# Another layout for the scratch tensor of the routing weights: pieces of four expert rows

## The chip, the cores and the metric

The kernel runs on one core of a Trainium2 chip. The metric is the device time of one launch in microseconds; several runs are compared by their median. Matrix products run on TensorE (PE), elementwise work on VectorE (DVE) and ScalarE (ACT), row gathers are issued by GpSimd (POOL), and most loads by SyncE (SP). Sixteen DMA engines move the data of all queues.

## The reference

Two transformer blocks over 512 tokens of width 1024, float32: the first with grouped attention, a gated convolution and a PEER layer, the second with sliding-window attention and a gated feed-forward layer. What bears on the change is the PEER layer, a mixture of 16384 experts of one hidden unit each:

```python
q = (xc @ wq).reshape(PEER_CHUNK, PEER_HEADS, 2, PEER_HALF)
s = jnp.einsum('thpd,hpnd->thpn', q, keys)          # 128 x 128 keys
s_top, i_top = lax.top_k(s, PEER_TOPK)              # 16 of each half
...
best_s, best_pos = lax.top_k(cand_s, PEER_TOPK)     # 16 experts of each head
w = jax.nn.softmax(best_s.astype(jnp.float32), axis=-1)
act = jax.nn.gelu(jnp.einsum('thkd,td->thk', jnp.take(u_tab, eid, axis=0), xc), approximate=False)
return jnp.einsum('thk,thkd->td', w * act, jnp.take(v_tab, eid, axis=0))
```

## The kernel before

The experts form a table of 128 rows of 128. For 384 of the 512 tokens (`TD`; `NTD` = 3 tiles of 128) the kernel computes the layer densely: for each expert row `b`, `stage_a` multiplies the tokens with the 128 vectors of the row (24 matmuls of three-part float32 into one PSUM bank of the two of `ps_mm`) and evicts the Gelu of it (`gt<-mm` on ACT), `stage_w` multiplies this with the routing weights of that row, and `stage_y` multiplies with the row's output vectors into the six banks `ys`. The last 128 tokens are done by gathers: GpSimd fetches the rows of `peer_u` and `peer_v` by index, and VectorE does the products.

The routing weights of the dense tokens come from `route` (VectorE) and `spread`. `spread` takes tokens in `NGRP` = 12 groups of `GW` = 32; for each token one matmul of two one-hot matrices gives its 128 x 128 table of weights in PSUM (`r`, the four banks of `ps_r`), and ACT copies these into the two staging tiles `wst[0]` and `wst[1]` (halves of the tile `rows1`, 64 expert rows each; the profile calls them `rows`). After the last eight tokens of a group, ACT issues one write of 1 MB out of each staging tile into the DRAM tensor `wr_d` (line 1357): 24 writes. `wr_d` is needed since the weights are made by tokens and used by expert rows.

This happens while PE also runs `lead(b)`: the first `LEAD` = 76 expert rows' `stage_a`, whose results ACT stores to the DRAM tensor `g_d` (line 1392). PE's matmuls for `spread` stand between those of `stage_a` in an order that is fixed when the program is built, by the costs and due times of the class `Pace`. After that `stage_a` for the other 52 rows and `stage_y` for all run by pairs of rows in the order `DSEQ`. Two steps ahead, `prepare` calls `load_wr(c)`, which loads the weights of `CH` = 4 expert rows for all 12 groups (768 KB, line 1409, two buffers, 32 loads on SyncE), and `load_g(b)`, which loads a stored `stage_a` (line 1414, also SyncE). The u and v tables come by loads of 1 MB each on SyncE (`raw`, line 271). Engines that go through the scheduler all have line 88 in the profile; the tile's name tells them apart.

Of the kernel before, what the change touches and what calls it, by code (L numbers as in the profile page):

```python
# [11 lines left out]
F32 = mybir.dt.float32  # L12
# [16 lines left out]
GW = 32  # L29
# [3 lines left out]
CH = 128 // GW  # L33
# [5 lines left out]
NGRP = TD // GW  # L39
# [25 lines left out]
class Pace:  # L65
# [119 lines left out]
    def need(self, tag, key="V"):  # L185
        for q in self.q[key]:
            while any(x[3] == tag for x in q):
                self.pop(key, q)
# [31 lines left out]
def tile_dit_peer_then_swa_block(ctx, tc, A, out, dbg=None):  # L220
    nc = tc.nc
# [19 lines left out]
    dram = ctx.enter_context(tc.tile_pool(name="dram", bufs=1, space=bass.MemoryType.DRAM))  # L241
# [107 lines left out]
    def later(items, tile, tag=None, first=False, deadline=1e9, key="V"):  # L349
        pace.later(items, tile, tag, 0 if first else 1, deadline, key)  # L350
# [183 lines left out]
    with ExitStack() as mx:  # L534
# [396 lines left out]
        for i in range(16):  # L931
# [18 lines left out]
            dst, c = (sga_d, sgc_d)[i // 8], i // 2 % 4  # L950
# [162 lines left out]


    sm = pool(ctx, "small2", 4)
    wr_d = dram.tile([NGRP, 128, 128 * GW], F32, name="wr_d")
    g_d = dram.tile([LEAD, 128, TD], F32, name="g_d")
    hp_ = ExitStack()
    gp = pool(hp_, "gp")
# [62 lines left out]
    if True:  # L1182
# [160 lines left out]
        def spread(t):  # L1343
            def group(g, g8, oa, ob):
                def f():
                    for u4 in range(2):
                        pw = ps_r.tile([128, 4, 128], F32, name="r", tag="r")
                        for u in range(4):
                            v = 4 * u4 + u
                            PE.matmul(pw[:, u, :], oa[:, v // 2, :, v % 2], ob[:, v // 2, :, v % 2], start=True, stop=True)  # L1350
                        n = 2 * (t * (128 // GW) + g)
                        o = 8 * g8 + 4 * u4
                        for i in range(2):
                            st = wst[i]
                            S.copy(st[:, :, o:o + 4], pw[:, :, i * 64:i * 64 + 64].rearrange("p t i -> p i t"))
                            if o == GW - 4:
                                nc.scalar.dma_start(wr_d[n // 2][:, i * 64 * GW:(i + 1) * 64 * GW],
                                                    st.rearrange("p i t -> p (i t)"))
                return f
            for g in range(128 // GW):  # L1360
                for g8 in range(GW // 8):
                    yield 2.9, lambda: cTs[t][1] if t in cTs else None
                    need(("cT", t), "PE")
                    n = ngrp[0]
                    ngrp[0] += 1
                    need(("oh", n - 2), "PE")
                    ci, cw = cTs[t]
                    oa = rw.tile([128, 4, 128, 2], F32, name="oa", tag="oab", bufs=4)
                    ob = rw.tile([128, 4, 128, 2], F32, name="ob", tag="oab", bufs=4)
                    eq = rw.tile([128, 4, 128, 2], BF, name="eq")  # L1370
                    ts_ = slice(g * GW + g8 * 8, g * GW + g8 * 8 + 8)
                    numbers = iota_u[:, None].to_broadcast([128, 4, 128, 2])

                    def eight(c):
                        return c[:, ts_].rearrange("p (a b) -> p a b", b=2)[:, :, None, :].to_broadcast([128, 4, 128, 2])
                    V.tensor_tensor(eq, numbers, eight(ci[:, 1]), op=ALU.is_equal)
                    V.tensor_tensor(oa, numbers, eight(ci[:, 0]), op=ALU.is_equal)
                    V.tensor_tensor(ob, eq, eight(cw), op=ALU.mult)
                    later([(1.8, group(g, g8, oa, ob))], ob, ("oh", n), key="PE")
# [20 lines left out]
    with ExitStack() as de:  # L1400
# [3 lines left out]
        wr, wfs = {}, {}  # L1404

        def load_wr(c):
            if c not in wr:
                wr[c] = dn.tile([128, NGRP, CH * GW], F32, name="wr", tag="wr", bufs=2)
                nc.sync.dma_start(wr[c], wr_d[:, :, c * CH * GW:(c + 1) * CH * GW].rearrange("g p c -> p g c"))
                pace.load(wr[c])  # L1410

        def load_g(b):
# [39 lines left out]
        def prepare(s):  # L1452

            if s >= steps:
                return
            j = DSEQ[s]
            for b in (2 * j, 2 * j + 1):
                load_wr(b // CH)
                if b < LEAD:
                    load_g(b)  # L1460
# [340 lines left out]
    with ExitStack() as ff:  # L1801
# [4 lines left out]
        for f0, f1 in FH:  # L1806
            f_hi = wk.tile([128, 12, T], F32R, name="f_hi", tag="f_hi", bufs=1)
            f_lo = wk.tile([128, 12, T], F32R, name="f_lo", tag="f_lo", bufs=1)
            for fc in range(f0 // 2, f1 // 2):
# [8 lines left out]
                for b in range(2):  # L1818
                    ps = block_T(uw, b, h_hi, h_lo) if fc else part_T(uw, b, h_hi, h_lo, slice(256, 512), early[2 + b])
                    V.tensor_tensor(sg[b], sg[b], ps, op=ALU.mult)  # L1820
                    i = 2 * fc + b - f0
# [105 lines left out]
```

## Time and profile before

| what | value |
|---|---|
| median of 3 runs | 2504.13 us (2501.92 to 2504.7) |
| the profiled execution, its own time | 2511.68 us |
| its span, first to last instruction | 2509.9 us |
| PE busy | 2417.8 us, 96% |
| VectorE, ACT, GpSimd busy | 71%, 40%, 14% |
| DMA | 491.27 MB, 196 GB/s mean |
| writes of `wr_d` (ACT) | 24 of 1024 KB, 860.1 to 1114.2 us |
| loads of `wr` (SyncE) | 32 of 768 KB, 1118.8 to 1890.8 us |

Times in the rows are microseconds from the start of the span unless ns is said. A row of instructions names the engine, the line, the operation and the tiles as out<-in; `ACTq` and `SPq` are the sequencers that issue DMAs. `q1` is the DMA queue of SyncE, `q10` that of ACT, `q0` that of the gathers. A group's idle time is that of the engine just ahead of it, with what ended it.

### The profile page before, as it was taken

How to read it: one execution, taken by the hardware profiler on the slowest of the kernel's cores; microseconds unless marked ns; L12 is line 12 of the kernel's file. 1: busy time of each engine (PE TensorE's matmuls, PEld its weight loads, DVE VectorE, ACT ScalarE, POOL GpSimd, SP SyncE). 2: the span in 40 equal slices, each digit the busy share in tenths (PEclk: the TensorE clock that was granted, in tenths of full speed). 3: DMA queues.
4: the chain of work that ended last, by engine and by line, in shares of the span. 5: the costliest groups of instructions: out<-in, count | busy, mean ns of one | idle time of the engine just before them, and what ended most of it. 6: DMA issues, size and time to landing. Idle time of an engine off the chain costs nothing. (4 is left out here: it accounts for less than half of the span.)

```text
span 2509.9 us, 33263 instructions
## 1 busy us (share of the span) xinstructions
PE 2417.8 (96%) x12953; PEld 2087.0 (83%) x12953; DVE 1781.7 (71%) x3259; ACT 1011.6 (40%) x1744; POOL 352.4 (14%) x278
## 2 busy tenths in 40 slices
PE   6999999998999999999999999999998999999998
PEld 4887878688899999998888888888887878888887
DVE  3899994555899999875877777778887487333333
ACT  4336556435334444443333333333335365321222
POOL 0000000000001112221433433334420000000000
PEclk9999999999999999999999999999999999999999
DMA  7222234344236677778998999999984211323221
GB/s 271 77 95 92 85 116 141 117 148 144 73 115 239 224 278 264 258 270 302 331 339 308 356 328 350 342 337 341 330 309 133 85 51 51 100 94 101 84 92 59
DMA packets 246318, 491.27 MB, mean 196 GB/s; under 512 B 12432, under 2 KB 177936, under 8 KB 226192
## 3 DMA queue, kind: packets, MB, share of 16 engines
q1 hardware_dynamic: 188032, 301.75, 35.0%
q0 software_dynamic: 36864, 134.23, 14.6%
q10 hardware_dynamic: 21264, 53.16, 5.8%
q8 instruction: 102, 1.67, 0.3%
q14 instruction: 56, 0.46, 0.1%
HBM read 440.60 MB, written 48.50 MB: 195 GB/s over the span
## 5 line engine op out<-in xcount | busy, mean ns | idle before, releaser
L88 DVE TENSOR_TENSOR wlo<-raw,whi 128x1024 fp32r<-128x1024 f32 (+1 forms) x420 | 494.1, 1216 | 236.4 <-ACT whi L88 235.7
L88 PE MATMUL mm<-hx_hi,whi 128*128 128x384 f32 (+2 forms) x1408 | 511.1, 363 | 16.1 <-ACT hx_hi L88 7.3
L88 ACT CAST whi<-raw 128x1024 fp32r<-128x1024 f32 (+1 forms) x420 | 418.3, 1045 | 200.6 <-PE pd L88 68.8
L88 PE MATMUL mm<-hx_lo,whi 128*128 128x384 f32 (+2 forms) x1408 | 497.5, 353 | 1.3 <-DVE hx_lo L88 1.3
L88 PE MATMUL mm<-hx_hi,wlo 128*128 128x384 f32 (+2 forms) x1408 | 496.8, 353 | 1.7 <-DVE wlo L88 1.7
L88 PE MATMUL y<-whi,wf 128*128 128x512 f32 x1536 | 428.3, 397 | 5.3 <-ACT whi L88 5.3
L88 PEld LDWEIGHTS y<-whi,wf 128*128 128x128 f32 x1536 | 288.6, 188 | 74.7 <-ACT whi L88 7.6
L1161 POOL DMA_INDIRECT rows<-in_peer_u_dram,eid x128 | 174.2, 1361 | 914.0 <-DVE eid L88 528.9
L88 PEld LDWEIGHTS mm<-hx_hi,whi 128*128 128x128 f32 x1408 | 267.0, 190 | 33.7 <-ACT hx_hi L88 8.7
L88 PEld LDWEIGHTS mm<-hx_hi,wlo 128*128 128x128 f32 x1408 | 266.7, 189 | 19.1 <-DVE wlo L88 3.3
L88 PEld LDWEIGHTS mm<-hx_lo,whi 128*128 128x128 f32 x1408 | 267.1, 190 | 15.6 <-DVE hx_lo L88 3.6
L88 PE MATMUL y<-wlo,wf 128*128 128x512 f32 x768 | 242.4, 397 | 4.1 <-DVE wlo L88 4.1
L1161 POOL DMA_INDIRECT rows<-in_peer_v_dram,eid x128 | 176.0, 1375 | 354.3 <-DVE yg L88 180.6
L88 PEld LDWEIGHTS y<-wlo,wf 128*128 128x128 f32 x768 | 144.1, 188 | 41.0 <-DVE wlo L88 6.7
L88 ACT CAST wf<-gt 128x384 fp32r<-128x384 f32 x128 | 66.1, 516 | 260.2 <-DVE gt L88 222.8
L88 DVE SCALAR_TENSOR_TENSOR cacc<-g,pcol,cacc 128x512 f32<-128x512 f32 x240 | 165.7, 751 | 0.0
L88 DVE SCALAR_TENSOR_TENSOR yg<-rows,cf,yg 128x1024 f32<-128x1024 f32 x127 | 162.7, 1281 | 0.9
L88 PE MATMUL mm<-h_hi,whi 128*128 128x512 f32 (+1 forms) x416 | 161.3, 388 | 0.0
L88 PE MATMUL mm<-h_lo,whi 128*128 128x512 f32 (+1 forms) x416 | 160.6, 386 | 0.0
L88 PE MATMUL mm<-h_hi,wlo 128*128 128x512 f32 (+1 forms) x416 | 160.6, 386 | 0.0
L88 DVE SCALAR_TENSOR_TENSOR rows<-rows,hg 128x1024 f32<-128x1024 f32 x128 | 154.2, 1220 | 0.0
L88 ACT ACTIVATE gt<-mm 128x384 f32<-128x384 f32 x128 | 63.9, 499 | 219.5 <-PE mm L88 199.7
(330 smaller groups left out, 3751.6 us busy)
## 6 DMA issues: line engine op xcount, KB each, us to landing
raw<-in_uT_dram SPq DMA_DIRECT2D x64, 1024.0 KB
raw<-in_peer_v_dram SPq DMA_DIRECT2D x64, 1024.0 KB
wr_d<-rows ACTq DMA_DIRECT2D x24, 1024.0 KB
wr<-wr_d SPq DMA_DIRECT2D x32, 768.0 KB
raw<-in_w_in_dram SPq DMA_DIRECT2D x22, 1024.0 KB
raw<-in_w_gu_dram SPq DMA_DIRECT2D x22, 1024.0 KB
raw<-in_w_mod_dram SPq DMA_DIRECT2D x18, 1024.0 KB
g_d<-gt ACTq DMA_DIRECT2D x76, 192.0 KB
```

Of the source, the lines that this page charges most:

```text
L88: return f(*a, **kw)
L1161: G.indirect_dma_start(out=r, out_offset=None, in_=A[tab], in_offset=bass.IndirectOffsetOnAxis(ap=eid[:, j:j + 1], axis=0))
```

## The change

`wr_d` gets the index of the piece of four expert rows (32 of them) first, then the partition, then the token group, then the 4 x 32 weights. A load of `wr` then reads one contiguous piece, 6 KB for each partition, where it read twelve runs of 512 bytes. A write of a staging tile goes to 16 pieces, 512 bytes for each partition and piece, where it was one run of 8 KB for each partition. The number and size of the transfers, who issues them and their place in the program are the same.

```diff
-    wr_d = dram.tile([NGRP, 128, 128 * GW], F32, name="wr_d")
+    wr_d = dram.tile([128 // CH, 128, NGRP, CH * GW], F32, name="wr_d")
...
                             if o == GW - 4:
-                                nc.scalar.dma_start(wr_d[n // 2][:, i * 64 * GW:(i + 1) * 64 * GW],
-                                                    st.rearrange("p i t -> p (i t)"))
+                                nc.scalar.dma_start(wr_d[i * 64 // CH:(i + 1) * 64 // CH, :, n // 2, :].rearrange("c p x -> p c x"),
+                                                    st.rearrange("p (c i) t -> p c (i t)", i=CH))
...
         def load_wr(c):
             if c not in wr:
                 wr[c] = dn.tile([128, NGRP, CH * GW], F32, name="wr", tag="wr", bufs=2)
-                nc.sync.dma_start(wr[c], wr_d[:, :, c * CH * GW:(c + 1) * CH * GW].rearrange("g p c -> p g c"))
+                nc.sync.dma_start(wr[c], wr_d[c])
                 pace.load(wr[c])
```

## Rows read from the trace of the kernel before

**Rows 1.** The page, busy time, share and instructions.
```profile
PE 2417.8 (96%) x12953; PEld 2087.0 (83%) x12953; DVE 1781.7 (71%) x3259; ACT 1011.6 (40%) x1744; POOL 352.4 (14%) x278
```
**Rows 2.** Windows; busy PE, PEld, DVE, ACT, POOL (instructions), clock, DMA share, GB/s.
```profile
860.00:1118.00 258.00, 254.24 (x1678) 252.84 (x1677) 226.93 (x305) 114.48 (x263) 46.80 (x29) 1.00 0.72 262
1118.00:1890.00 772.00, 756.27 (x3604) 650.29 (x3603) 591.38 (x761) 269.02 (x375) 288.00 (x214) 0.99 0.90 329
```
**Rows 3.** DMA queues, 1074.5 to 1076.8 us; packets, MB, share of 16 engines.
```profile
q10 hardware_dynamic: 125, 1.02, 106.7%
```
**Rows 4.** DMA queues, 1179.5 to 1181 us.
```profile
q1 hardware_dynamic: 833, 0.42, 99.5%
```
**Rows 5.** Tile `wr_d`: its DMA issues (ns min/median/max), who waited (us, times).
```profile
L1409 SPq DMA_DIRECT2D wr<-wr_d x32: 377/434/1848, 1118.8 to 1890.8; - x32
L1357 ACTq DMA_DIRECT2D wr_d<-rows x24: 326/326/361, 860.1 to 1114.2; - x24
...
  ACT rows L88: 58.6, 19
```
**Rows 6.** Timeline of ACT, 1073.5 to 1083.5 us; start, duration, idle before.
```profile
1073.68 0.33 ACTq L1357 DMA_DIRECT2D wr_d<-rows  x1
...
1074.45 0.33 ACTq L1357 DMA_DIRECT2D wr_d<-rows  x1
1077.68 0.37 ACT L88 COPY rows<-r 128x256 f32<-128x256 f32 x1 [3.26 <-DMA wr_d<-rows]
1082.13 0.93 ACT L88 COPY rows<-r 128x256 f32<-128x256 f32 x3 [4.07 <-DMA wr_d<-rows]
1082.93 0.53 ACT L88 ACTIVATE gt<-mm 128x384 f32<-128x384 f32 x1
```
**Rows 7.** Timeline of ACT behind the second wait of five other pairs.
```profile
869.93 0.93 ACT L88 COPY rows<-r 128x256 f32<-128x256 f32 x3 [2.01 <-DMA wr_d<-rows]
...
906.56 0.53 ACT L88 ACTIVATE gt<-mm 128x384 f32<-128x384 f32 x1
...
983.35 0.52 ACT L88 ACTIVATE gt<-mm 128x384 f32<-128x384 f32 x1
...
1024.48 0.53 ACT L88 ACTIVATE gt<-mm 128x384 f32<-128x384 f32 x1
...
1101.51 0.93 ACT L88 COPY rows<-r 128x256 f32<-128x256 f32 x3 [2.81 <-DMA wr_d<-rows]
```
**Rows 8.** Timeline of PE: the first matmul that needs what ACT freed.
```profile
871.24 0.63 PE L88 MATMUL r<-ob,oa 128*128 128x128 f32 x4
...
909.39 0.42 PE L88 MATMUL mm<-hx_hi,whi 128*128 128x384 f32 x1
...
984.05 0.34 PE L88 MATMUL mm<-hx_hi,whi 128*128 128x384 f32 x1
...
1025.05 0.44 PE L88 MATMUL mm<-hx_hi,whi 128*128 128x384 f32 x1 [0.43 <-ACT gt L88]
...
1083.51 0.44 PE L88 MATMUL mm<-hx_hi,whi 128*128 128x384 f32 x1
...
1102.24 0.63 PE L88 MATMUL r<-ob,oa 128*128 128x128 f32 x4
```
**Rows 9.** Waits, 1118 to 1145 us; us in total, times, longest.
```profile
ACT gt L88 <- DMA wr<-wr_d: 12.2, 1, 12.2
...
PE mm L88 <- ACT gt L88: 5.0, 1, 5.0
```
**Rows 10.** DMA queues, 1127 to 1132 us.
```profile
q0 software_dynamic: 421, 1.54, 75.6%
q1 hardware_dynamic: 477, 0.24, 16.3%
```
**Rows 11.** Waits of DVE, 1145 to 1890 us.
```profile
DVE gt L88 <- DMA gt<-g_d: 28.4, 13, 7.0
```
**Rows 12.** Tile `g_d`: its loads' issues, ns min/median/max.
```profile
L1414 SPq DMA_DIRECT2D gt<-g_d x76: 320/453/6783, 1119.3 to 1900.5; - x76
```

## The prediction

> **What bounds the kernel now.** I read the page first: TensorE (PE) is busy for 96% of the span [rows 1], so a microsecond counts only where it makes PE stand still. Then the table by windows, for the two stretches in which the scratch tensor `wr_d` is used [rows 2]. While it is written (860 to 1118 us) PE is busy 254.24 of 258 us, 3.8 us idle, with the DMA engines at 0.72. While it is read (1118 to 1890 us) PE is busy 756.27 of 772 us, 15.7 us idle, with the DMA engines at 0.90. So the reading stretch has at most 15.7 us to give back, however much faster its loads become, and the writing stretch has next to no idle time of PE: what is lost there shows at once, unless slack between the engines takes it.
>
> Next the view of the tensor itself [rows 5]. The 24 writes are issued by ScalarE (ACT), and ACT is also who waits for them: 58.6 us in 19 waits. The reason is in `spread`: each of the two staging tiles `wst` exists once, so the copy that begins the next group of 32 tokens must wait until the write out of that tile has landed. The 32 loads are issued by SyncE, and their one long waiter is ACT again, 12.2 us at the first of them [rows 9].
>
> Third, one pair of writes on ACT's timeline [rows 6]: first write issued at 1073.68, second at 1074.45; the first copy of the next group gets its tile at 1077.68 after 3.26 us of idling, the second at 1082.13 after 4.07 more. So 8.45 us pass from the first issue to the end of the second wait. Behind that copy stands the Gelu eviction at 1082.93, and PE starts its next block, in the bank that this eviction frees, at 1083.51 [rows 8]. The eviction ended at 1083.46: the slack is 0.05 us. This reading, who on PE comes right behind the second wait and with how much room, is the one that decides the case, so I made it for all twelve pairs. Six are shown [rows 7, 8]; the copies of `rows` there are three in 0.93 us, so the first ends some 0.4 us after its start:
> - pair of 860 us: copy ends about 870.3, PE's `r` matmul at 871.24: 0.9 us
> - pair of 898 us: Gelu ends 907.09, PE at 909.39: 2.3 us
> - pair of 974 us: 983.87 against 984.05: 0.2 us
> - pair of 1014 us: 1025.01 against 1025.05, and PE has already idled 0.43 us for it: 0.05 us
> - pair of 1073 us: 0.05 us
> - pair of 1091 us: about 1101.9 against 1102.24: 0.35 us
>
> The other six have 2.8 us or more, or no copy waiting.
>
> **The change part by part.** *Writes.* A write of 1 MB went out as 128 packets of 8 KB, eight for each of the 16 DMA engines; now it is 2048 packets of 512 bytes, 128 for each. The price of both sizes is in the trace, in windows where nothing else runs. 8 KB writes: 125 packets at 106.7% of 16 engines over 2.3 us, so 314 ns each [rows 3]. 512-byte packets, of the old loads: 833 at 99.5% over 1.5 us, so 28.7 ns each [rows 4]. Per KB that is 39 against 57 ns. A pair of writes therefore takes 2 x 8 x 314 ns = 5.0 us of every engine before and 2 x 128 x 28.7 ns = 7.35 us after: 2.3 us more. That reads are as dear as writes is assumed; no 512-byte write stands in the trace.
>
> How much later does the second wait end? Of the 8.45 us, 5.0 are the pair's own transfer and 3.4 are the start, the landing and others' packets. If those 3.4 stay, the wait ends 2.3 us later; if all of it grows with the transfer (7.35/5.0), 3.9 us later. The row gathers on the third queue go on all through the stretch, so a longer window catches more of them, but start and landing don't grow: I take 3.0. The issue itself gets dearer: a three-level pattern took 434 ns (the old loads) against 326 for the plain one [rows 5], 0.1 us for each of two writes. So the wait ends 3.2 us later, between 2.5 and 4.1.
>
> Queued behind the waiting copy on ACT are the other copies of that group, the Gelu evictions, their `g_d` stores and the `whi` casts of the next weights; PE waits for the first three kinds as soon as the slack is gone. The shift beyond the slack is then PE's, pair by pair, at 3.2: 2.3 + 0.9 + 3.0 + 3.15 + 3.15 + 2.85 = **15.4 us lost**. At 2.5 it is 11.2; at 4.1 it is 20.8, and 2.3 more from pairs among the other six.
>
> *Loads.* Each load of 768 KB was 1536 packets of 512 bytes and becomes 128 of 6 KB. Between the two prices 6 KB take some 236 ns (an estimate, at the 8 KB packet's rate): 32 loads cost 32 x 96 x 28.7 ns = 88 us of all engines before and 60 after. The 28 us are what the writes gain in length (24 x (128 x 28.7 - 8 x 314) ns = 28 us): the DMA work is moved from the stretch at 0.90 to the one at 0.72, not removed. What the shorter loads release is read from who waited. The large one is the first load, issued at 1118.84 us. From 1127 to 1132 us the gathers (q0) hold 75.6% of the engines with 421 packets, while the queue of the load gets 477 packets through in 16.3% [rows 10]: about one small packet for one of 4 KB. So the load took until about 1138, and ACT stood 12.2 us for it in the middle of its evictions; PE stood 5.0 us [rows 9]. With eight packets of 6 KB for each engine, taken in turn with as many of the gathers, it needs 8 x (0.24 + 0.16) = 3.2 us. That stall goes: **5.0 us gained**. What is late next there is the last pair of writes itself, 3 us later than now, ahead of the first load; the evictions around it held PE up only in that one wait, so I count nothing for it.
>
> After 1145 us the loads of `g_d`, which SyncE issues right behind a load of `wr`, are waited for by VectorE: 28.4 us in 13 waits [rows 11]. No idle time of PE in this stretch is put down to the products behind them; 10.7 us of the 15.7 are left as the cap. I take **1.5 us gained**, between 0 and 10.7.
>
> *Nothing else.* SyncE's own issue gets cheaper (434 to 326 ns, 32 times), hidden, since SyncE mostly waits for free buffers. Computation, tiles and order are untouched.
>
> **Sum.** 15.4 - 5.0 - 1.5 = +8.9 us. The profiled execution took 2511.68 us (span 2509.9 and 1.8 around it); with the change 2520.6. It lies 7.5 us over the median of the runs, 2504.13, and none of that is in these terms, so the forecast for a median is **2513.0 us**.
>
> **The rivals.**
> 1. *Small writes run at the large ones' rate.* Then the waits end 0.2 us later, for the issues alone, PE loses about 0.3 us at the three tightest pairs, and the gains stand: 0.3 - 6.5 = -6.2, 2497.9 us; with the whole idle time of the reading stretch given back, 2489. It decides as soon as the waits grow by less than about 1 us. Against it speak the 28.7 ns: at the large packets' rate 512 bytes would take 19.6 [rows 3, 4]. For it: those were reads, into SBUF.
> The Trainium skill (DMA: Bandwidth & Descriptors, Specifications) puts the least transfer for line rate at 512 bytes, so by that page this rival would be the case; by it the sum would be the -6.2 of this rival. The trace so far does not agree: 0.42 MB of 512-byte loads in 1.5 us of full engines is 280 GB/s, against 1.02 MB of 8 KB writes in 2.3 us, 443 GB/s [rows 3, 4].
> 2. *Small writes are dearer than small reads, or hold ACT in the issue.* SyncE's issues of `g_d` loads take 0.45 us as a rule and up to 6.8 [rows 12], and the long ones stand behind a load of 512-byte packets: the issuer is held until much of that load is through. The second write, 2048 packets behind 2048, would hold ACT in the same way, and the evictions behind it. If the second wait ends 6 us later, the six pairs lose 5.1 + 3.7 + 5.8 + 5.95 + 5.95 + 5.65 = 32.2 and the others about 9: 41 - 6.5 = +35, 2539 us; at 6.8, the longest issue, some 2546.
> 3. *The two halves cancel.* Waits 1.7 to 2.5 us longer, or more than 1.5 us from the reading stretch: within 5 us of 2504. For it speaks that the DMA time moved is the same on both sides.
>
> **How the numbers follow.** Forecast 0.45 (own range 2508.8 to 2521), rival 1 0.17, rival 2 0.23, rival 3 0.15. The range goes from 2496 to 2545: it leaves out the better half of rival 1 and the worst third of rival 2. Of a measurement of this kernel 0.2%, 5 us, can be told from no change (the three runs lie 2.8 us apart). Slower is the forecast but for its lowest edge, and rival 2: 0.66; faster is rival 1: 0.17; the rest, 0.17, is the same.
>
> **What would show it.** In the profile after: ACT's wait for the `wr_d` writes up from 58.6 us to some 95; packets of 512 bytes on q10 near 28.7 ns; PE idle in the writing stretch up from 3.8 us to some 19, with waits for `gt` and `rows` copies; no long wait of ACT for the first load and no 5 us of PE near 1135; PE idle after that smaller by about a microsecond or two. The prediction is wrong if the writes land as early as now, if ACT's issues grow by microseconds, or if the reading stretch gives back more than its waits suggest.

## The result and the profile after

The changed kernel takes 2538.24 us (median of 5, 2530.25 to 2539.83) against 2504.13 us: a ratio of 1.0128 (95% interval 1.011 to 1.0145), 34 us slower by the medians. The forecast was 2513.0, 8.9 us slower, with a range up to 2545.

First the windows, cut at the first and the last write of `wr_d` and at the end of the reading, of both kernels (length; busy PE, PEld, DVE, ACT, POOL with instructions; clock; DMA share; GB/s). Before:

```profile
0.00:860.10 860.10, 810.69 (x4829) 698.04 (x4830) 665.00 (x1606) 398.48 (x649) 17.71 (x36) 0.98 0.41 136
860.10:1114.20 254.10, 250.34 (x1655) 248.94 (x1654) 226.83 (x305) 113.65 (x261) 46.70 (x29) 1.00 0.71 261
1114.20:1900.80 786.60, 770.87 (x3677) 662.90 (x3676) 599.57 (x776) 275.09 (x388) 288.00 (x214) 0.99 0.90 327
```

After:

```profile
0.00:855.80 855.80, 804.32 (x4829) 692.85 (x4830) 664.52 (x1606) 397.48 (x649) 17.59 (x36) 0.99 0.41 137
855.80:1147.60 291.80, 265.07 (x1656) 262.04 (x1655) 226.76 (x305) 113.27 (x260) 45.84 (x29) 0.94 0.70 227
1147.60:1927.50 779.90, 769.80 (x3676) 662.58 (x3675) 599.74 (x776) 274.58 (x387) 284.43 (x214) 1.00 0.89 330
```

The matmuls of each stretch are the same (1655 and 1656, 3677 and 3676), so the lengths can be subtracted. Writing: 37.7 us longer, of which PE idles 23.0 more (26.7 for 3.8) and is *busy* 14.7 more for the same matmuls, at a granted clock of 0.94 for 1.00. Reading: 6.7 us shorter, 5.6 of it idle time (10.1 for 15.7). Ahead of the first write the profiled execution of before was 4.3 us longer, at 0.98 for 0.99; the change has nothing there. The tails are equal (609.1 and 609.0). Together +26.6 us between the two spans (2509.9 and 2536.5); the profiled execution of before lay 7.5 us over its median, that of after on it, which makes the 34.

The tile `wr_d` after (issues in ns min/median/max; who waited), and the stores of `g_d` that ACT issues behind the writes:

```profile
L1409 SPq DMA_DIRECT2D wr<-wr_d x32: 319/432/652, 1154.4 to 1917.5; - x32
L1357 ACTq DMA_DIRECT2D wr_d<-rows x24: 377/485/4340, 855.8 to 1147.6; - x24
...
  ACT rows L88: 60.6, 15
```
```profile
L1392 ACTq DMA_DIRECT2D g_d<-gt x76: 326/327/6161, 723.9 to 1174.9; - x76
```

ACT's wait for the writes is hardly longer than in [rows 5], 60.6 for 58.6 us. The rest of what was expected there has changed its name: a write's issue, 361 ns at most before, now takes up to 4.3 us, and the store behind it up to 6.2 (1.1 at most before). In the waits of ACT, 855 to 1160 us (total, times, longest), it stands as "issue":

```profile
ACT rows L88 <- DMA wr_d<-rows: 60.6, 15, 9.1
...
ACT gt L88 <- issue: 20.8, 6, 4.5
ACT whi L88 <- issue: 7.0, 2, 3.8
```

What PE waited for, 855 to 1150 us:

```profile
PE mm L88 <- ACT gt L88: 16.3, 4, 5.2
PE r L88 <- DVE ob L88: 6.9, 3, 2.7
PE mm L88 <- DVE wlo L88: 2.1, 1, 2.1
PE r L88 <- ACT rows L88: 1.4, 2, 0.9
```

One pair of writes on ACT's timeline (that of 898 us in [rows 7]) and the matmul that it held up:

```profile
898.60 0.38 ACTq L1357 DMA_DIRECT2D wr_d<-rows  x1
...
899.41 1.15 ACTq L1357 DMA_DIRECT2D wr_d<-rows  x1
...
903.31 0.38 ACT L88 COPY rows<-r 128x256 f32<-128x256 f32 x1 [0.71 <-DMA wr_d<-rows]
912.78 0.92 ACT L88 COPY rows<-r 128x256 f32<-128x256 f32 x3 [9.09 <-DMA wr_d<-rows]
913.58 0.52 ACT L88 ACTIVATE gt<-mm 128x384 f32<-128x384 f32 x1
```
```profile
914.15 0.69 PE L88 MATMUL mm<-hx_hi,whi 128*128 128x384 f32 x1 [4.43 <-ACT gt L88]
```

From the first issue to the second copy 14.2 us pass, where before it was 7.4: the Gelu eviction stands behind that copy and PE behind the eviction, as the prediction read it. What it did not read is seen in windows of 2 us over the same gap (the eighth column is the clock):

```profile
910.00:912.00 2.00, 0.00 (x0) 0.00 (x0) 2.00 (x3) 0.00 (x0) 0.00 (x0) 1.00 1.01 357
912.00:914.00 2.00, 0.00 (x0) 0.00 (x0) 0.91 (x1) 1.22 (x4) 0.00 (x0) 0.74 0.05 15
914.00:916.00 2.00, 1.85 (x6) 1.85 (x7) 0.00 (x0) 1.59 (x6) 0.00 (x0) 0.50 0.31 107
916.00:918.00 2.00, 2.00 (x11) 2.00 (x10) 0.41 (x1) 1.59 (x3) 0.00 (x0) 0.50 0.27 98
...
920.00:922.00 2.00, 2.00 (x15) 2.00 (x14) 2.00 (x4) 0.54 (x2) 0.00 (x0) 1.00 0.49 86
```

PE stands still, the clock falls to 0.50 (1.2 of 2.4 GHz), and stays there while PE works again. The same sixteen routing matmuls, ahead of the gap and behind it, on PE's timeline:

```profile
907.68 2.04 PE L88 MATMUL r<-ob,oa 128*128 128x128 f32 x16
...
916.24 3.62 PE L88 MATMUL r<-ob,oa 128*128 128x128 f32 x16
```

So a gap of 4.4 us costs more than 4.4 us. The Trainium skill (TensorE: Matmul & The Clock Gate, Part 1) describes this: an array that has been idle falls to the 1.2 GHz level and returns only after it has been busy again. The trace agrees: 0.50 from 914 to 918 us with PE at work, 1.00 from 920.

### The profile page after: what moved, and what is told of

It reads as the page before. It is cut to its first block, busy times and chain, and to the rows that moved or that the text cites. A ratio compares the mean times of both kernels' runs of the same rounds, so it can differ in the third digit from the quotient of the medians.

```text
span 2536.5 us, 33263 instructions
## 1 busy us (share of the span) xinstructions
PE 2425.1 (96%) x12953; PEld 2094.5 (83%) x12953; DVE 1781.1 (70%) x3259; ACT 1009.1 (40%) x1744; POOL 347.9 (14%) x278
## 5 line engine op out<-in xcount | busy, mean ns | idle before, releaser
L88 PE MATMUL mm<-hx_hi,whi 128*128 128x384 f32 (+2 forms) x1408 | 512.6, 364 | 28.4 <-ACT gt L88 17.9
```

Source lines behind the costliest of these rows:

```text
L88: return f(*a, **kw)
```

## The experiments

Ratios are against the kernel before, run on the same chip between the runs of the experiment. In the edits long expressions are given a name or shortened, and `...` stands for what is left out.

**1. The two halves apart.** The loads alone, over the writes of before:

```diff
-nc.sync.dma_start(wr[c], wr_d[:, :, c * CH * GW:(c + 1) * CH * GW].rearrange("g p c -> p g c"))
+N = 128 * NGRP * CH * GW
+nc.sync.dma_start(wr[c].rearrange("p g x -> p (g x)"),
+                  wr_d.rearrange("g p x -> (g p x)")[c * N:(c + 1) * N].rearrange("(p x) -> p x", p=128))
```

> The 24 writes are those of before (8 KB runs); each load of 768 KB takes one contiguous piece of the scratch tensor, 128 packets of 6 KB, so it fetches other weights of the same size. Theory A (the loss of the change lies in the writing stretch alone: the writes land later, PE idles, and the granted clock falls behind it; the loads only gain): 5 to 8 us faster than before, about 2498; ACT's wait of 12.2 us for the first load and PE's 5.0 us behind it are gone, PE idle from the last write to 1900 us down from 15.7 to about 10, and the writing stretch as before (3.8 us idle, clock 1.00). Theory B (the first load is late because of the gathers and whatever stands ahead of it, not because of its 512-byte packets): the waits stay and the time is within 2 us of before.

Measured: 0.9961 (0.995 to 0.9973), some 10 us faster. The reading stretch holds 8.5 us of idle time. The writing stretch was expected as before, 3.8 us, but has 8.3:

```profile
858.20:1118.40 260.20, 251.94 (x1655) 250.54 (x1654) 226.70 (x305) 113.95 (x261) 46.77 (x29) 0.99 0.71 259
1118.40:1896.90 778.50, 770.05 (x3677) 663.53 (x3676) 600.02 (x776) 274.52 (x387) 283.75 (x214) 1.00 0.88 329
```

Of these 8.3 us one gap makes 4.7, with the writes of before:

```profile
1087.04 0.69 PE L88 MATMUL mm<-hx_hi,whi 128*128 128x384 f32 x1 [4.74 <-ACT gt L88]
```

It stands behind the pair of 1072 us, whose second copy came 13.2 us after the first issue, where before it came after 8.45. Between these two points lie 2.07 MB of gathers and SyncE's loads, where before there were 0.79. So a tile can come free late with the old writes too, and a few microseconds of idle time in this stretch tell nothing of the writes.

One thing limits this run: the piece that its first load takes holds the first token group only, so that load left at 1112.1 us, ahead of the last write. In experiment 3, where the first load must wait for later writes, the reading stretch has 8.4 us of idle time, so the gain doesn't hang on it.

The writes alone, in the changed layout, and loads of twelve 512-byte runs:

```diff
-nc.sync.dma_start(wr[c], wr_d[c])
+nc.sync.dma_start(wr[c], wr_d.rearrange("c p g x -> (c p g x)")
+                  .rearrange("(g p x) -> p g x", p=128, g=NGRP)[:, :, c * CH * GW:(c + 1) * CH * GW])
```

> The 24 writes are those of the change (512-byte runs); each load takes twelve runs of 512 bytes for each partition out of the same memory as before, so it fetches other weights of the same size. Theory A (the two halves add): what the change cost plus what the loads gained, 34 + 6 = 40 us slower than before, about 2544; writing stretch of some 291 us with about 26 us of PE idle at a clock of 0.94, and the 5.0 us of PE behind the first load again. Theory B (the loads gain nothing by themselves): 2538, as the whole change.

Measured: 1.0141 (1.0122 to 1.0161), 35 us slower. The writing stretch is that of the change, the reading stretch has its idle time back (17.5 us):

```profile
855.00:1146.90 291.90, 264.40 (x1656) 261.39 (x1655) 226.78 (x305) 113.28 (x260) 45.84 (x29) 0.94 0.71 229
1146.90:1938.40 791.50, 774.00 (x3676) 663.84 (x3676) 599.29 (x776) 274.39 (x387) 283.86 (x214) 0.99 0.90 324
```

The two ratios multiply to 1.010, just under the 1.011 to 1.0145 of the change and within the intervals of the two. The loss sits in the writes, the gain in the loads.

**2. Does idle time alone lower the clock?** The kernel before, its DMAs untouched, with ACT kept busy behind the second copy that waits for a staging tile:

```diff
 S.copy(st[:, :, o:o + 4], pw[:, :, i * 64:i * 64 + 64].rearrange("p t i -> p i t"))
+if i == 1 and o == 0 and n // 2 > 0:
+    for _ in range(8):
+        nc.scalar.copy(dly, hg[:, 0:512])
```

> The kernel before with eight copies of 128x512 (0.54 us each by the rate of the 128x1024 casts, 4.3 us together) on ACT behind the second copy that waits for a staging tile, eleven times; no DMA is touched, nothing is left out. Theory A (PE's idle time is what lowers the clock): PE idle of the writing stretch up by some 22 to 27 us and the granted clock there down from 1.00 to about 0.94, so PE's busy time for the same matmuls up by another 12 to 16 us: 36 to 41 us slower, about 2541. Theory B (the clock or the longer busy time of the changed kernel comes with its DMA traffic): the same idle time, clock 1.00, busy time as before: 22 to 27 us slower, about 2528.

Measured: 1.02 (1.0181 to 1.0218), some 50 us slower. The delay came out larger than planned (the eight copies take 5.2 us), and PE idled 40.1 us:

```profile
856.30:1160.90 304.60, 264.48 (x1655) 261.08 (x1654) 227.34 (x305) 166.44 (x348) 45.84 (x29) 0.94 0.60 218
```

PE is busy 264.5 us for the 1655 matmuls that took 250.3, at 0.94, with the old DMAs. So a longer busy time needs no small packets: idle gaps bring it. The rate is not the same: here 36.3 us more of idle time cost 14.1 us, in the changed kernel 23.0 cost 14.7.

**3. How long a pair of writes takes, and in how many packets.** Four kernels. Writes in runs of 2 KB (512 packets), with contiguous loads:

```diff
-nc.scalar.dma_start(wr_d[i * 64 // CH:(i + 1) * 64 // CH, :, n // 2, :].rearrange("c p x -> p c x"),
-                    st.rearrange("p (c i) t -> p c (i t)", i=CH))
+wr8 = wr_d.rearrange("c p g x -> (c p g x)").rearrange("(c p g x) -> c p g x", c=8, p=128, g=NGRP)
+nc.scalar.dma_start(wr8[i * 4:(i + 1) * 4, :, n // 2, :].rearrange("c p x -> p c x"),
+                    st.rearrange("p (c i) t -> p c (i t)", i=16))
```

> As the change, but each write goes out in runs of 2 KB (16 expert rows) instead of 512 bytes, 512 packets for 1 MB; the contiguous loads then fetch other weights of the same size. Theory A (the price is one for each packet and one for each byte: 314 ns for 8 KB and 27.2 for 512 bytes make 8 ns and 38 ns for each KB, so 2 KB take some 85 ns, a write 2.7 us against 2.5 and 3.5): the waits end at most 0.7 us later than before, PE loses 1 to 3 us, and the gain of the loads stays: 2 to 6 us faster than before, about 2500. Theory B (any write broken into more runs than one for each partition is held up, by its issue or in its queue): over 2520.

Measured: 0.9994 (0.9984 to 1.0004), not the gain expected. The price was right: between 1076.5 and 1078.5 us

```profile
q10 hardware_dynamic: 398, 0.82, 104.8%
```

is 84 ns for 2 KB. But the second copies came 1.2 us later on the mean, not 0.7 at most, and with 10.0 us of idle time the writing stretch gave back what the loads gained (8.4 us of idle time in the reading).

Writes as long as the change's in large packets, with the old loads:

```diff
 nc.scalar.dma_start(wr_d[n // 2][:, i * 64 * GW:(i + 1) * 64 * GW], ...)
+nc.scalar.dma_start(more_d[n // 2 % 2 * 2 + i], st[:, 0:30, :].rearrange("p i t -> p (i t)"))
```

> The kernel before, with its writes in 8 KB runs, but behind each of the 24 writes another of 0.47 MB out of the same staging tile (128 packets of 3.75 KB) to a tensor that nobody reads: a pair then takes some 2 x (8 x 314 + 8 x 147) ns = 7.4 us of each DMA engine, as a pair of the change (7.0 to 7.35), in 32 packets for each engine instead of 256. Nothing is left out. Theory A (what costs is how late the staging tiles come free, whatever the packets): PE idle of the writing stretch near the change's 26.7 us, clock about 0.94, no gain of the loads: 30 to 42 us slower, about 2543. Theory C (what costs is ACT held in the issue of DMAs with many packets): ACT's issues stay below 1.5 us and the time is at most 8 us above before.

Measured: 1.0174 (1.0145 to 1.0202), 44 us slower, a little over theory A's bound:

```profile
857.60:1165.10 307.50, 268.51 (x1658) 263.65 (x1657) 226.98 (x305) 113.63 (x261) 45.86 (x29) 0.93 0.68 252
```
```profile
ACT rows L88 <- DMA more_d<-rows: 96.9, 20, 9.1
```

The loss of the change, and more, without one small packet more. The issues are held less (2.0 us at most, a little over the 1.5 of theory C), and the wait stands under its own name, 96.9 us.

The changed kernel with half of each write left out:

```diff
-nc.scalar.dma_start(wr_d[i * 64 // CH:(i + 1) * 64 // CH, :, n // 2, :].rearrange("c p x -> p c x"),
-                    st.rearrange("p (c i) t -> p c (i t)", i=CH))
+nc.scalar.dma_start(wr_d[i * 64 // CH:i * 64 // CH + 8, :, n // 2, :].rearrange("c p x -> p c x"),
+                    st[:, 0:8 * CH, :].rearrange("p (c i) t -> p c (i t)", i=CH))
...
-nc.sync.dma_start(wr[c], wr_d[c])
+nc.sync.dma_start(wr[c], wr_d[c // 16 * 16 + c % 8])
```

> The changed kernel, but each write takes only the first 32 of its 64 expert rows (1024 packets of 512 bytes, 0.5 MB), and the loads fetch the pieces that are written, so half of the weights are left out of the scratch tensor and others are used in their place. A pair of writes takes 2 x 64 x 27.2 ns = 3.5 us of each DMA engine, less than the 5.0 us of before, in as small packets as the change. Theory A (the loss goes with how late the staging tiles come free): no gap of PE over 1 us behind a landing wait, clock 1.00 in the writing stretch, and the loads' gain stays: 6 to 10 us faster than before, about 0.997. Theory C (small packets cost by themselves, by ACT's issues or otherwise): still over 10 us slower.

Measured: 0.9936 (0.9918 to 0.9955), 16 us faster, more than expected; in small packets, and PE hardly idles in the writing stretch:

```profile
859.30:1108.70 249.40, 248.66 (x1655) 248.02 (x1654) 226.54 (x305) 113.83 (x260) 46.50 (x29) 1.00 0.66 220
```

And with a quarter left out (12 pieces of the 16 instead of 8), so that a pair takes about as long as before, in 192 packets for each engine:

> The changed kernel, but each write takes 48 of its 64 expert rows (1536 packets of 512 bytes, 96 for each DMA engine), and the loads fetch pieces that are written, so a quarter of the weights is left out of the scratch tensor and others are used in their place. A pair of writes takes 2 x 96 x 27.2 ns = 5.2 us of each engine, as long as that of before (5.0) or that in 2 KB runs (5.4), in 192 packets for each engine instead of 16 or 64. Theory A (only the length counts): PE idle of the writing stretch 4 to 10 us, clock 0.99 to 1.00, ratio 0.996 to 1.000. Theory C (ACT held in the issue adds to it): issues of the second write or of the store behind it of 1 us and more, PE idle above 12 us, ratio above 1.002.

Measured: 0.9983 (0.9973 to 0.9994), as theory A has it: 8.8 us of idle time, clock 1.00. ACT was still held: a write's issue took up to 1.3 us, that of a store behind the writes up to 5.5:

```profile
L1392 ACTq DMA_DIRECT2D g_d<-gt x76: 326/327/5503, 725.8 to 1142.1; - x76
```

So issues held this long can cost little.

Side by side, with the mean time from a pair's first issue to its second waiting copy (ten pairs, ACT's timeline), and the length of a pair's own transfer. This is reckoned from the rate at which writes of that size went through with the engines to themselves: 348 GB/s for 512 bytes (below), 407 for 2 KB, 443 for 8 KB [rows 3]; the 3.75 KB writes are put between the last two, an estimate. The expectations reckoned with the time of a packet instead, which makes the pairs longer:

| kernel | pair, us | packets per engine | issue to copy, us | PE idle, writing | PE busy, writing | ratio |
|---|---|---|---|---|---|---|
| half left out | 3.0 | 128 | 7.0 | 0.7 | 248.7 | 0.9936 |
| before (old loads) | 4.7 | 16 | 9.1 | 3.8 | 250.3 | 1 |
| quarter left out | 4.5 | 192 | 9.4 | 8.8 | 250.3 | 0.9983 |
| 2 KB runs | 5.2 | 64 | 10.3 | 10.0 | 252.1 | 0.9994 |
| the change | 6.0 | 256 | 11.7 | 26.7 | 265.1 | 1.0128 |
| long writes (old loads) | 7.1 | 32 | 13.6 | 39.0 | 268.5 | 1.0174 |

Idle time rises with the time from issue to copy, and hardly with the number of packets. That time rises by more than the transfer does, as others' packets fall into a longer pair (see below). Between 4 and 10 us the idle time is no measure of the writes: the loads alone, with the writes of before, had 8.3.

**4. Another order.** If the eviction stands behind the landing, it can be put ahead of it; the second line follows each write:

```diff
-later([(1.8, group(g, g8, oa, ob))], ob, ("oh", n), key="PE")
+later([(1.8, group(g, g8, oa, ob))],
+      ob if g8 else (lambda ob=ob: ob if pace.t["PE"] >= landing[0] else None), ("oh", n), key="PE")
...
+landing[0] = pace.t["S"] + 4.0
```

> The changed kernel; when the order is planned, the first eight tokens of the next group aren't taken before 4 us of planned time after the second write, so that in all pairs a Gelu eviction stands on ACT ahead of the copies that wait for the staging tiles (in the changed kernel four of the pairs that waste most have none there). Nothing is left out. Theory A (the loss is the evictions queued behind the landing wait): the four gaps of PE of 2.5 to 5.2 us shrink to under 1 us each, PE idle of the writing stretch 26.7 to about 10, clock 0.94 to about 0.98, 20 to 30 us less than the changed kernel: about 2513. Theory C (ACT is held in the issues, ahead of the evictions): the eviction that now comes first is behind the held issue too, and the time stays over 2530.

Measured: 1.0068 (1.0045 to 1.0091), 17 us slower than before and so half of the loss. That is between the two theories: the idle time fell to 22.4 us, not to about 10, and the clock is 0.96. No matmul waits for a Gelu any more, but in 858 to 1144 us the routing matmuls wait for the copies instead, whose banks they need:

```profile
PE r L88 <- ACT rows L88: 12.3, 7, 2.6
PE r L88 <- DVE ob L88: 6.7, 5, 2.0
PE mm L88 <- DVE wlo L88: 3.3, 1, 3.3
```

The next eight tokens put off as well (not before 10 us):

> The changed kernel in an order in which the first eight tokens behind the second write are not taken before 4 us of planned time and the next eight not before 10 us, so that PE has a block of the first stage between the matmuls whose copies wait for the landing. Nothing is left out. Theory A: the waits of the routing matmuls for the copies (2 us each in the order with one delay) shrink as well: 8 to 15 us less than that order's 1.0068 of before, so 1.000 to 1.003; if the loss there was the held issue instead, about 1.007 again.

Measured: 1.0094 (1.0072 to 1.0116): the expectation failed. The waits went to VectorE's one-hot matrices (`r` for `ob`, 15.5 us in 8 waits). VectorE makes them late because it first waits for ACT's `whi` casts, 48.3 us in this stretch for 16.7 before, and several of these casts now stand behind held issues:

```profile
ACT whi L88 <- issue: 17.2, 4, 5.7
```

So in this order a part of the cost is the held issue's; how much was not measured apart. The loss can be moved among the engines in this stretch; a place where it vanishes was not found.

The same order with the old layout, twice:

> The same order with the layout of before (8 KB writes, 512-byte loads). Theory A: the writing stretch had 3.8 us of PE idle to give back, so 0 to 4 us faster than before, about 2502. With the kernel of the new layout in the same order about 8 us behind it or less, the layout's own cost in this order is read from the two.

> The old layout in the order with one delay once more, to see whether its 0.9985 (0.9971 to 1.0000) holds: 0.997 to 1.000 if it does.

Measured: 0.9985 (0.9971 to 1.0000) and 0.9986 (0.9971 to 1.0001): some 4 us faster both times, the best version found that computes everything, at the edge of what can be told from none. It did not come from where it was expected: the writing stretch has 4.0 and 4.3 us of idle time, no less than the 3.8 of before. And in this order the new layout costs about 21 us (1.0068 for 0.9985), not the 8 at most that were expected.

**5. The first load by itself.**

```diff
+if i == 0:
+    nc.scalar.dma_start(wr0_d[:, n // 2, :], st[:, 0:CH, :].rearrange("p i t -> p (i t)"))
...
+nc.sync.dma_start(wr[c], wr0_d if c == 0 else wr_d[...])
```

> The layout of before but for the first four expert rows, which lie in a tensor of their own by partitions (128 packets of 512 bytes in each first write of a pair, the other 60 expert rows in runs of 7.5 KB); the first load is 128 packets of 6 KB, the other 31 as before. Nothing is left out. Theory A (the first load is late for its 512-byte packets against the gathers'): its wait of 12.2 us on ACT and PE's 5.0 us go, a pair of writes grows by 0.2 us and one issue of 0.33 us: 2 to 5 us faster than before, about 2501 to 2502. Theory B (the first load is late for what stands ahead of it): no change beyond 2 us, or slower by the issues.

Measured: 1.001 (0.9996 to 1.0024), no gain. PE's 5.0 us of [rows 9] are gone, and yet the reading stretch has as much idle time as before:

```profile
1118.30:1906.60 788.30, 772.28 (x3674) 662.97 (x3673) 598.87 (x776) 273.99 (x387) 289.73 (x214) 1.00 0.89 326
```
```profile
PE mm L88 <- DVE wlo L88: 6.3, 6, 1.4
```

16.0 us, with six waits for `wlo` that before were two, of 0.8 us together. And the writing stretch, where each pair has one DMA more, went to 8.1 us.

## Why the prediction came out as it did

The direction, the place and the chain of waits were right; the size was short by 25 us. The measured time lies in the range only because of rival 2; the forecast's own range ended at 2521. Step by step:

- *Price of the small packets.* Forecast 28.7 ns, and with it 2.3 us more for a pair. From 1033.5 to 1036 us after, 512-byte writes have the engines to themselves (0.87 MB, 348 GB/s):

```profile
q10 hardware_dynamic: 1701, 0.87, 114.8%
```

  A packet's time is 27.0 ns, but a share over 100% says that packets overlap: one went through every 23.5 ns on each engine. The same holds for the 106.7% of [rows 3], 294 ns for 314, and not for the 99.5% of the loads in [rows 4]. So a pair takes 6.0 us for 4.7, 1.3 more and not 2.3, and small writes are somewhat cheaper than small reads (348 GB/s for 280). They stay dearer than large ones (443), so rival 1 falls. By the page of the Trainium skill named there (DMA: Bandwidth & Descriptors, Specifications) 512 bytes would be enough for line rate; the trace does not agree: 348 GB/s with 512 bytes, 407 with 2 KB, 443 with 8 KB.

- *The second wait ends 3.2 us later.* On the mean of ten pairs it is 2.6 (9.1 to 11.7), within 2.5 to 4.1, but that is luck: single pairs lie between 1.7 us earlier and 6.8 later. They go with what else falls into the pair's time. Three pairs have as many megabytes of gathers and SyncE's loads between first issue and copy as before, within 0.1; they end 0.7, 0.9 and 1.4 us later, about the 1.3 of the transfer. Four pairs have 0.75 to 1.8 MB more and end 4.5 to 6.8 us later; one has 0.85 MB less and ends 1.7 us earlier; the last two, with 0.24 MB less and more, end 1.7 and 1.95 us later. In the pair of 898 us, after (898.6 to 912.8 us) and before (898.4 to 905.8 us, where `q1` has nothing):

```profile
q0 software_dynamic: 288, 1.05, 26.0%
q1 hardware_dynamic: 144, 1.05, 17.5%
```
```profile
q0 software_dynamic: 70, 0.29, 10.2%
```

  A longer pair catches more of them, as the prediction says, but it did not reckon with over a megabyte in one pair and none in the next. Whether the longer writes alone bring them there was not tested; in the run with the loads alone one such pair arose with the old writes.

- *15.4 us lost at six pairs.* PE's gaps there are 0.5, 4.4, 4.2, 2.5, 5.2 and 0 us, 16.8 together, where 2.3, 0.9, 3.0, 3.15, 3.15 and 2.85 were forecast. The rule, shift less slack, holds: with each pair's own shift (1.4, 6.8, 4.5, 1.95, 5.7 and -1.7 us) in place of 3.2 it gives 0.5, 4.5, 4.3, 1.9, 5.65 and 0. That the total came out near the forecast is luck. Another 9.9 us lie elsewhere (`r` for `ob` 6.9, `wlo` 2.1, one copy 0.9), where before they were 3.2. The prediction named the `whi` casts among what is queued on ACT, and then let PE wait only "for the first three kinds". But VectorE waits for the casts, 43.9 us for 16.7 before, and comes late with the one-hot matrices and with `wlo`, for which PE waits.

- *The failed step: that the loss is the idle time.* "The shift beyond the slack is then PE's, pair by pair" counts the gaps and nothing behind them. The gaps also lowered the clock, and the same matmuls took 14.7 us longer. This is the largest term of the case that the sum did not have; experiment 2 shows that gaps alone can bring as much. The trace of before showed it in small, behind the 5.0 us gap of [rows 9]:

```profile
1135.00:1145.00 10.00, 5.68 (x25) 5.68 (x26) 3.98 (x5) 2.87 (x4) 0.43 (x1) 0.83 0.85 335
```

- *The loads.* Forecast 6.5 us, measured 5.6 of idle time. By the names of PE's waits 3.4 of these are the `gt` evictions around the first load (1.6 us in 2 waits for 5.0 in 1), 1.6 are `wlo` and 0.6 `whi`, not far from the 5.0 and 1.5 of the forecast. But the terms don't stand by themselves: experiment 5 took the first load's stall away and gained nothing, since waits for `wlo` came in its place. With all 32 loads in 6 KB runs they did not, and VectorE's waits for the `g_d` loads behind them fell from 28.4 us in 13 [rows 11] to

```profile
DVE gt L88 <- DMA gt<-g_d: 15.3, 7, 3.7
```

  (41.8 us in experiment 5). That the one follows from the other is not shown.

- *Rival 2* named the time (2539), and a part of the cause. The packets are not dearer than small reads, and the landing was 6 us later in two of the ten pairs (5.7 and 6.8), but not on the mean. ACT was held in the issue, as it says, up to 6.2 us (issues that grow by microseconds are a sign, by the prediction's own words, that it is wrong), and two of the new gaps stand behind that and behind no landing:

```profile
883.95 2.00 ACT L88 CAST whi<-raw 128x1024 fp32r<-128x1024 f32 x2 [3.75 <-issue]
...
931.19 0.22 ACT L88 ACTIVATE cf<-dots 128x16 f32<-128x16 f32 x1 [2.76 <-issue]
```
```profile
885.03 2.36 DVE L88 TENSOR_TENSOR wlo<-raw,whi 128x1024 fp32r<-128x1024 f32 x2 [4.76 <-ACT whi L88]
...
931.44 0.18 DVE L88 TENSOR_TENSOR cf<-cf,wg 128x16 f32<-128x16 f32 x1 [8.71 <-ACT cf L88]
```
```profile
891.56 3.02 PE L88 MATMUL r<-ob,oa 128*128 128x128 f32 x16 [2.11 <-DVE ob L88]
...
940.10 0.58 PE L88 MATMUL mm<-hx_hi,wlo 128*128 128x384 f32 x1 [2.10 <-DVE wlo L88]
```

  Before, PE had no gap at either place. So some 4 of the 23.0 us are the held issue's. The larger part, 16.3 us in four gaps, lies behind landings, at pairs whose second write was issued within 1.2 us. The run that would part the two, small packets of the full length from a queue that holds nobody, was not tried.

- *The profiled execution.* Its 7.5 us over the median were carried as an offset. 4.3 of them lie ahead of the first write, where nothing differs, and were not there in the profiled execution after.

With the terms as measured the sum is 23.0 + 14.7 - 6.7 = 31.0 us, inside the 27.5 to 36.3 that the interval of the ratio allows.

## What to carry to other kernels

A new layout for a scratch tensor moves the small runs from one side to the other; ask which side has the waiter with no room, not which side moves more bytes. Where an in-order engine frees a buffer that it must itself refill, time the transfer against the slack of whoever stands behind it, pair by pair, and look up what other queues will send in the longer time: here that moved the single pairs more than the transfer did. List every engine that waits for the held one, not only the bottleneck. And price a gap of TensorE at its length plus what the clock takes behind it: here 23.0 us of new gaps cost 14.7 us more.

## What was not expected of the hardware

- An issue on ACT that takes 0.33 us took up to 4.3 (a write) and 6.2 us (a store of 192 KB behind two writes of 2048 packets each; a store took 1.1 at most before). The time moved from the wait for the DMA into "issue", so the wait alone hid it: 60.6 us after 58.6.
- Not every gap has the same price. The order with two delays had 27.0 us of idle time in the writing stretch, as the change, but in more and shorter gaps, and its clock was 0.98 and its busy time 258.8 us, where the change has 0.94 and 265.1:

```profile
857.60:1143.40 285.80, 258.83 (x1659) 253.10 (x1658) 226.16 (x305) 114.13 (x261) 54.17 (x28) 0.98 0.72 233
```
